# Hybrid decoder layer: another order of the mixer's projections, and the second half of the out-projection on VectorE

## The chip, the core and the metric

One Trainium2 chip, one core. The metric is the device time of one execution in microseconds; the median of three runs is given. The engines are TensorE (PE; PEld is its weight load), VectorE (DVE), ScalarE (ACT), GpSimd (POOL) and SyncE (SP), which issues the DMAs.

## The reference

All is float32; 512 tokens, width 1024. The layer is a SwiGLU FFN (half step), a mixer, and a second SwiGLU FFN:

```python
x = x + 0.5 * swiglu(rms_norm(x))                       # width 2816
proj = rms_norm(x) @ w_in                               # 1024 x 2560
xr, gate, q, k, v = split(proj, 512 columns each)
y_rnn = rg_lru(xr) * gelu(gate)                         # conv of 4, two block-diagonal gates, scan over time
q, k = rms_norm per head (8 heads of 64)
z = q @ k.T;  w = exp(log_sigmoid(z) + sum of log_sigmoid(-z) over later keys), causal
y_att = w @ v
y = concat(rms_norm(y_rnn), rms_norm(y_att))
x = x + y @ w_out
x = x + 0.5 * swiglu(rms_norm(x))
```

The recurrent half makes, for each channel, h[t] = a[t] h[t-1] + b[t] with a and b from two sigmoid gates of the convolved xr.

## The kernel before

Tokens lie along the free axis (512), channels on the 128 partitions, so x is eight tiles of 128x512. Each float32 matmul is three (`mm3`, lines 136 to 139): both operands are split into a rounded high part (ScalarE) and the rest (VectorE), and high x high, high x low and low x high are summed in a PSUM bank. `weights` loads a weight tile with one DMA from SP, then splits it; there are 3 buffers for the raw tile and 4 for each part. `Normed.add` splits x times a gain into `xh` and `xl`; the norm's factor is applied later, when the product is read. `Normed.square` has ScalarE square x and GpSimd add up the squares; four matmuls with a column of ones sum these over the partitions (`rsqrt`), and four transposes spread the result over a tile `rb` (`spread`).

The order in which each engine issues is made at build time by a planner: it goes through the program with a model of the engines, and of the instructions that the model has ready it takes the earliest in program order; `weights_early` moves an instruction 200 places forward. A tile with a tag takes one of that tag's buffers when its first instruction is placed, and one whose buffers are all held waits until one is released, while later instructions may pass it. `tc.issue_after(ins)` holds back, behind `ins`, the instructions of the block that are on the engine of `ins`, and no others.

In the mixer the eight PSUM banks are six with the tag "b" and two with the tag "y". `project(j)` makes block j of xr and gate (two banks "b", 48 matmuls); `convolve(j)` reads them, makes the convolution `xc`, its two parts `xch` and `xcl`, and the gelu `gel`; `gate(j)` makes the two gate products (6 matmuls, two banks) and the sigmoids from them. `recur` needs all four gates: exponentials, a square root, VectorE's scans, and a product on GpSimd into `gel`. `rnn_out` splits `gel` into `yrh` and `yrl`. `project_qkv` makes q, k or v for four groups of 128 tokens in four banks, 32 groups of three matmuls; after a given number of groups it calls what `between` says. For k the first two of the four banks have the tag "y". `norm_heads` norms the heads of q or k (square, sum, a power on GpSimd, a product into `nat`, which releases the bank), `turn` transposes `nat` on TensorE and splits it. The order before is: block 0, block 1, block 2, gate 0, block 3, gate 1, q with gates 2 and 3 inside, k with the recurrence and q's transposes inside, v with `rnn_out` and k's transposes inside.

In the attention, `weigh` makes scores and weights for a pair of heads, `turn_weights` transposes them, `attend` multiplies by v. The out-projection is made in two halves: `project_out(k, 0, ...)` for the recurrent half, put in between steps of the attention, and `project_out(k, 1, ...)` for the attention's half, for k = 0 to 7 at the end. Each is 12 matmuls, a product with `rb` on VectorE (`yo`, two buffers) and an addition into x[k] on GpSimd. After each of the second half, `done(k)` splits the new x[k] into `xh_b` and `xl_b` for the second FFN, whose banks take over those of the attention; last come the eight squares.

Of the kernel before, what the change touches and what calls it, by code (L numbers as in the profile page):

```python
# [8 lines left out]
F32 = mybir.dt.float32  # L9
F32R = mybir.dt.float32r  # L10
BF16 = mybir.dt.bfloat16
AF = mybir.ActivationFunctionType
# [3 lines left out]
P = 128  # L16
T = 512
D = 1024
KD = D // P
DFF = 2816  # L20
NF = DFF // P
DR = 512
# [27 lines left out]
def hybrid_layer_kernel(  # L50
# [17 lines left out]
    nc = tc.nc  # L68
# [21 lines left out]
    def bank(name, tag="b"):  # L90
        return banks["pool"].tile([P, T], F32, tag=tag, name=name, bufs=banks["tags"][tag])
# [25 lines left out]
    x = [xpool.tile([P, T], F32, tag=f"x{k}", name=f"x{k}") for k in range(KD)]  # L117


    def weights(src, name, n=KD * P):  # L120
        raw = wpool.tile([P, n], F32, tag="wr", name=f"r_{name}")
        nc.sync.dma_start(raw, src)
        return parts(raw, name, n)

    def parts(raw, name, n):
# [6 lines left out]
    def weights_early(*args):  # L132
        with tc.high_priority(offset=200):
            return weights(*args)
# [7 lines left out]
    class Normed:  # L142
# [5 lines left out]
        def add(self, xk, gain, j):  # L148
            n = self.name
            h = xpool.tile([P, T], F32R, tag="xh", name=f"xh_{n}{j}", bufs=8)  # L150
            nc.scalar.activation(h, xk, AF.Copy, scale=gain)
            l = xpool.tile([P, T], F32R, tag="xl", name=f"xl_{n}{j}", bufs=8)
            low = nc.vector.scalar_tensor_tensor(
                l, xk, gain, f32(h), op0=ALU.mult, op1=ALU.subtract
            )
            self.h[j], self.l[j] = h, l
            return low

        def square(self, xk, j):
            n = self.name  # L160
# [337 lines left out]
    rp = rnn.enter_context(tc.tile_pool(name="rnn", bufs=1, reuse_waits="tile"))  # L498
# [4 lines left out]
    def project(j, between=None):  # L503

        ws = [weights_early(w_rg[c], f"{n}{j}") for c, n in ((j, "xr"), (NJ + j, "ga"))]
        pts = [bank(f"p{n}{j}") for n in ("xr", "ga")]
        order = [(i, k) for i in range(2) for k in range(KD)]
        if j == 0:
            order = [(i, k) for k in ORDER for i in range(2)]
        for i, k in order:  # L510
            s = slice(k * P, (k + 1) * P)
            (wh, wl), ks = ws[i], [kk for ii, kk in order if ii == i]
            mm3(pts[i], wh[:, s], wl[:, s], nm.h[k], nm.l[k], k == ks[0], k == ks[-1])
            if between and (i, k) == order[KD - 1]:
                between()
        return pts

    def convolve(j, pr, pg):
        xr = rp.tile([P, T + 3], F32, tag="xr", name=f"xr{j}")
        nc.vector.memset(xr[:, 0:3], 0.0)  # L520
        nc.vector.tensor_mul(xr[:, 3:], pr, nm.rb)
        g = rp.tile([P, T], F32, tag=f"gel{j}", name=f"gel{j}")
        nc.vector.tensor_mul(g, pg, nm.rb)
        xc = rp.tile([P, T], F32, tag="xc", name=f"xc{j}", bufs=2)
        nc.gpsimd.tensor_scalar(
            xc, xr[:, 3:], v1(C_CW + 3 * NJ + j), v1(C_CB + j), op0=ALU.mult, op1=ALU.add
        )
        for w in range(3):
            nc.vector.scalar_tensor_tensor(
                xc, xr[:, w : w + T], v1(C_CW + w * NJ + j), xc, op0=ALU.mult, op1=ALU.add  # L530
            )
        xch = rp.tile([P, T], F32R, tag="xch", name=f"xch{j}", bufs=2)
        nc.scalar.copy(xch, xc)
        xcl = rp.tile([P, T], F32R, tag="xcl", name=f"xcl{j}", bufs=2)
        nc.vector.tensor_sub(xcl, xc, f32(xch))
        conv.append((xc, xch, xcl))

        g2 = rp.tile([P, T], F32, tag="g2", name=f"g2{j}")
        nc.scalar.activation(g2, g, AF.Square)
        k0 = 2.0 * (2.0 / 3.141592653589793) ** 0.5  # L540
        nc.gpsimd.tensor_scalar(g2, g2, k0 * 0.044715, k0, op0=ALU.mult, op1=ALU.add)
        nc.gpsimd.tensor_mul(g2, g2, g)
        nc.scalar.activation(g2, g2, AF.Sigmoid)
        nc.gpsimd.tensor_mul(g, g, g2)
        gel.append(g)

    def gate(j):
        xc, xch, xcl = conv[j]
        s = slice(j * P, (j + 1) * P)
        pa = bank(f"pa{j}")  # L550
        mm3(pa, bah[:, s], bal[:, s], xch, xcl, True, True)
        px = bank(f"px{j}")
        mm3(px, bxh[:, s], bxl[:, s], xch, xcl, True, True)

        nc.scalar.activation(dec[:, j, :], pa, AF.Sigmoid, bias=v1(C_BA + j))
        nc.scalar.activation(tau[:, j, :], dec[:, j, :], AF.Tanh, scale=half_c[:, j : j + 1])
        i = rp.tile([P, T], F32, tag=f"ix{j}", name=f"ix{j}")
        box["gate"] = nc.scalar.activation(i, px, AF.Sigmoid, bias=v1(C_BX + j))
        nc.gpsimd.tensor_mul(i, i, xc)
        ix.append(i)  # L560

    yrh, yrl = [], []
    box = {}

    yn = Normed("r")
# [36 lines left out]
    v = []  # L602
# [22 lines left out]
    def norm_heads(n, pts):  # L625
        nats = []
        for b in range(NB):
            rb = nm.r[:, b : b + 1]
            sq = rp.tile([P, DR], F32, tag="nsq", name=f"nsq{n}{b}", bufs=1)
            nc.scalar.activation(sq, pts[b], AF.Square, scale=rb)  # L630
            m = stat.tile([P, NH], F32, tag="m8", name=f"m8{n}{b}")
            nc.vector.tensor_reduce(m, heads(sq), axis=mybir.AxisListType.X, op=ALU.add)
            nc.vector.tensor_scalar(m, m, 1.0 / HD, EPS, op0=ALU.mult, op1=ALU.add)
            r = stat.tile([P, NH], F32, tag="r8", name=f"r8{n}{b}")
            nc.gpsimd.tensor_tensor(r, m, mhalf, op=ALU.pow)
            nat = rp.tile([P, DR], F32, tag=("xch", "xcl")[b % 2], name=f"nat{n}{b}", bufs=2)
            nc.vector.scalar_tensor_tensor(
                heads(nat),
                heads(pts[b]),
                rb,  # L640
                r.unsqueeze(2).to_broadcast([P, NH, HD]),
                op0=ALU.mult,
                op1=ALU.mult,
            )
            nats.append(nat)
        return nats
# [16 lines left out]
    pj = [project(0)]  # L663
# [2 lines left out]
    bah, bal = blockdiag(bd_a, "a")  # L666
    bxh, bxl = blockdiag(bd_x, "x")
    convolve(0, *pj[0])
    pj.append(project(2))
    convolve(1, *pj[1])  # L670
    gate(0)
    pj.append(project(3))
    convolve(2, *pj[2])
    gate(1)
    convolve(3, *pj[3])
    pq = project_qkv(0, "q", {8: lambda: gate(2), 16: lambda: gate(3)})
    nq = norm_heads("q", pq)
    pk = project_qkv(1, "k", {8: recur, 24: lambda: turn("q", nq)})
    nk = norm_heads("k", pk)
    pv = project_qkv(2, "v", {8: rnn_out, 27: lambda: turn("k", nk)})  # L680
    for b in range(NB):
        rb = nm.r[:, b : b + 1]
        v.append(mp.tile([P, DR], F32, tag=f"v{b}", name=f"v{b}", bufs=1))
# [3 lines left out]
    psum("att", z=4, w=3, y=1)  # L687


    def project_out(k, c, yh, yl, norm, tag, after=None):  # L690
        wh, wl = weights_early(w_out[k, :, c * DR : (c + 1) * DR], f"o{c}_{k}", DR)
        pt = bank(f"po{c}_{k}", tag)
        with tc.issue_after(after.ins) if after else nullcontext():
            for j in range(NJ):
                s = slice(j * P, (j + 1) * P)
                mm3(pt, wh[:, s], wl[:, s], yh[j], yl[j], j == 0, j == NJ - 1)
        tmp = ap.tile([P, T], F32, tag="yo", name=f"yo{c}_{k}", bufs=2)
        nc.vector.tensor_mul(tmp, pt, norm.rb)  # L698
        nc.gpsimd.tensor_add(x[k], x[k], tmp)

# [2 lines left out]
    with tc.tile_pool(name="att", bufs=2, reuse_waits="tile") as ap:  # L705
        beta = {}
        yah, yal = [], []
# [99 lines left out]

        yn.rsqrt(DR)
        yn.spread()
        project_out(0, 0, yrh, yrl, yn, "w")  # L810
        todo = 1
        ahead()
        ahead()
        for j, pair in enumerate(pairs):
            ws = []
            for h in pair:
                ws.append(ap.tile([P, 4 * W + P], F32, tag="wt", name=f"wt{h}", bufs=4))
            for qbs in ((3,), (2,), (1, 0)):
                for h, w in zip(pair, ws):
                    turn_weights(qbs, h, w)  # L820
                    if steps in WEIGH:
                        ahead()
                    if steps in FILL:
                        project_out(todo, 0, yrh, yrl, yn, "z")
                        todo += 1
                    steps += 1
            py = bank(f"py{j}", "y")
            attend(pair, py, ws)
            take(j, py)
        na.rsqrt(DR)  # L830
        na.spread()
        for k, step in zip(range(todo, KD), REST):
            project_out(k, 0, yrh, yrl, yn, "z", turns[step])
        n2 = Normed("b")
        done = into(n2, C_G2, squares=False)
        for k in range(KD):

            after = None if k < 2 else na.summed if k == 2 else na.spreading
            project_out(k, 1, yah, yal, na, "zw"[k % 2], after)
            done(k)  # L840
        with tc.issue_after(done.last.ins):
            for k in range(KD):
# [99 lines left out]
```

## Time and profile before

| what | us |
|---|---|
| median of three runs | 949.89 (949.12 to 950.03) |
| the profiled execution | 950.52 |
| its span, first to last instruction | 948.7 |
| TensorE busy | 927.4 |
| VectorE busy | 676.1 |
| ScalarE busy | 374.7 |
| GpSimd busy | 125.2 |

The mean granted clock of TensorE is 0.992 of its full rate. Busy time of TensorE counts overlapping matmuls once; a matmul of 512 columns is shown as 0.39 us but the next goes off earlier. The mixer lies between about 364 and 581 us: projections to 489, attention to 558, then the second half of the out-projection.

### The profile page before, as it was taken

How to read it: one execution, taken by the hardware profiler on the slowest of the kernel's cores; microseconds unless marked ns; L12 is line 12 of the kernel's file. 1: busy time of each engine (PE TensorE's matmuls, PEld its weight loads, DVE VectorE, ACT ScalarE, POOL GpSimd, SP SyncE). 2: the span in 40 equal slices, each digit the busy share in tenths (PEclk: the TensorE clock that was granted, in tenths of full speed). 3: DMA queues.
4: the chain of work that ended last, by engine and by line, in shares of the span. 5: the costliest groups of instructions: out<-in, count | busy, mean ns of one | idle time of the engine just before them, and what ended most of it. 6: DMA issues, size and time to landing. Idle time of an engine off the chain costs nothing.

```text
span 948.7 us, 12527 instructions
## 1 busy us (share of the span) xinstructions
PE 927.4 (98%) x4906; PEld 786.1 (83%) x4906; DVE 676.1 (71%) x997; ACT 374.7 (39%) x532; POOL 125.2 (13%) x87
## 2 busy tenths in 40 slices
PE   8999999999999999999899997999999999999998
PEld 6888988898889888888776575888988899889987
DVE  7687867686768559766859849287776777677753
ACT  7233333333333335446457546143333324233430
POOL 4000000000000005633802139100000000000000
PEclk9999999999999999999999998999999999999999
DMA  7430443035201513321110013421153125212312
GB/s 245 178 111 1 142 148 109 3 123 166 89 23 67 156 67 111 128 74 66 56 56 23 23 67 121 168 89 45 67 179 107 49 68 178 89 67 67 111 45 89
DMA packets 27131, 89.45 MB, mean 94 GB/s; under 512 B 3136, under 2 KB 5440, under 8 KB 27072
## 3 DMA queue, kind: packets, MB, share of 16 engines
q1 hardware_dynamic: 27072, 88.65, 27.2%
q8 instruction: 39, 0.64, 0.3%
q14 instruction: 20, 0.16, 0.1%
HBM read 86.54 MB, written 2.10 MB: 93 GB/s over the span
## 4 chain that ended last, share of the span: by engine, by line
PE 84%; DVE 7%; DMA 4%; issue 2%; POOL 1%; ACT 1%; SPq 0%; DVEq 0%; POOLq 0%; ACTq 0%
PE pdb L343 8%; PE pda L343 8%; PE pga L137 5%; PE pga L139 5%; PE pga L138 5%; PE pub L137 4%; PE pub L139 4%; PE pub L138 4%; PE pgb L137 4%; PE pgb L139 4%; PE pgb L138 4%; PE pua L137 4%; PE pua L138 4%; PE pua L139 4%; DVE rest L743 1%
## 5 line engine op out<-in xcount | busy, mean ns | idle before, releaser
L137 PE MATMUL pub<-xh_b,h_ub 128*128 128x512 f32 x176 | 69.2, 393 | 6.2 <-DVE yo L698 6.2
L343 PE MATMUL pda<-bha,l_da 128*128 128x256 f32 x252 | 70.5, 284 | 1.0 <-DVE l_da L129 1.0
L343 PE MATMUL pdb<-bhb,l_db 128*128 128x256 f32 x252 | 70.5, 284 | 0.9 <-DVE l_db L129 0.8
L343 PE MATMUL pdb<-bhb,h_db 128*128 128x256 f32 x252 | 71.3, 284 | 0.0
L343 PE MATMUL pda<-bha,h_da 128*128 128x256 f32 x252 | 71.2, 284 | 0.0
L343 PE MATMUL pda<-bla,h_da 128*128 128x256 f32 x252 | 71.0, 283 | 0.0
L343 PE MATMUL pdb<-blb,h_db 128*128 128x256 f32 x252 | 71.0, 283 | 0.0
L139 PE MATMUL pub<-xh_b,l_ub 128*128 128x512 f32 x176 | 69.0, 392 | 0.0
L138 PE MATMUL pub<-xl_b,h_ub 128*128 128x512 f32 x176 | 69.0, 392 | 0.0
L137 PE MATMUL pgb<-xh_b,h_gb 128*128 128x512 f32 x176 | 68.9, 392 | 0.0
L139 PE MATMUL pgb<-xh_b,l_gb 128*128 128x512 f32 x176 | 68.8, 391 | 0.0
L138 PE MATMUL pgb<-xl_b,h_gb 128*128 128x512 f32 x176 | 68.7, 391 | 0.0
L137 PE MATMUL pga<-xh_a,h_ga 128*128 128x512 f32 x160 | 62.4, 390 | 0.0
L137 PE MATMUL pua<-xh_a,h_ua 128*128 128x512 f32 x160 | 62.3, 390 | 0.0
L139 PE MATMUL pga<-xh_a,l_ga 128*128 128x512 f32 x160 | 62.3, 389 | 0.0
L138 PE MATMUL pga<-xl_a,h_ga 128*128 128x512 f32 x160 | 62.3, 389 | 0.0
L139 PE MATMUL pua<-xh_a,l_ua 128*128 128x512 f32 x160 | 62.3, 389 | 0.0
L138 PE MATMUL pua<-xl_a,h_ua 128*128 128x512 f32 x160 | 62.2, 389 | 0.0
L167 POOL TENSOR_TENSOR sqa_m<-sqa_m,sq_m 128x512 f32<-128x512 f32 x7 | 11.8, 1682 | 326.8 <-issue 322.9
L343 PEld LDWEIGHTS pda<-bha,l_da 128*128 128x128 f32 x252 | 47.9, 192 | 1.4 <-DVE l_da L129 1.4
L246 DVE TENSOR_TENSOR uub<-pub,rb_b 128x512 f32<-128x512 f32 x22 | 15.2, 690 | 47.3 <-PE pub L139 47.3
L343 PEld LDWEIGHTS pdb<-bhb,l_db 128*128 128x128 f32 x252 | 47.8, 192 | 1.3 <-DVE l_db L129 1.3
(316 smaller groups left out, 2474.3 us busy)
## 6 DMA issues: line engine op xcount, KB each, us to landing
r_gb<-in_wg SPq DMA_DIRECT2D x22, 512.0 KB, 3.2
r_ub<-in_wu SPq DMA_DIRECT2D x22, 512.0 KB, 3.3
r_ga<-in_wg SPq DMA_DIRECT2D x20, 512.0 KB, 3.2
r_ua<-in_wu SPq DMA_DIRECT2D x20, 512.0 KB, 3.6
rda<-in_wd SPq DMA_DIRECT2D x12, 768.0 KB, 5.1
rdb<-in_wd SPq DMA_DIRECT2D x12, 768.0 KB, 4.8
r_o<-in_w_out SPq DMA_DIRECT2D x16, 256.0 KB, 2.7
x<-in_xT SPq DMA_DIRECT2D x8, 256.0 KB, 4.5
```

Source lines behind the costliest of these rows:

```text
L137: nc.tensor.matmul(out_, wh, ah, start=start, stop=False)
L138: nc.tensor.matmul(out_, wh, al, start=False, stop=False)
L139: nc.tensor.matmul(out_, wl, ah, start=False, stop=stop)
L167: nc.gpsimd.tensor_add(self.acc, self.acc, sq)
L246: nc.vector.tensor_mul(u, pu, rb)
L343: nc.tensor.matmul(pt, p[:, s], a, start=start and i == 0 and q == 0, stop=i == m - 1 and q == 2, skip_group_check=True,)
L743: nc.vector.tensor_tensor_scan(rest[:, c : c + n - 1][:, ::-1], s[:, c + 1 : c + n][:, ::-1], zero.to_broadcast([P, n - 1]), 1.0, op0=ALU. ...
```

## The change

The projections run in the order block 0, block 1, q (with gates 0 and 1 inside), block 2, the transposes of q, block 3 (with gate 2 inside), k (with gate 3 and the recurrence inside, after eight groups), v (with `rnn_out` after twelve groups instead of eight, and k's transposes). The gates' banks have the tag "y" in place of "b". `nat` has a tag of its own with three buffers, in place of two each of `xch` and `xcl`. In the second half of the out-projection VectorE, not GpSimd, adds into x[k], and the weights of two k come with one DMA and are split in one go. `Normed.add` returns its ScalarE instruction, so that the last `issue_after` holds the eight squares behind the last `xh_b`.

```diff
-    def weights(src, name, n=KD * P):
+    def weights(src, name, n=KD * P, rows=1):
         raw = wpool.tile([P, n], F32, tag="wr", name=f"r_{name}")
-        nc.sync.dma_start(raw, src)
+        nc.sync.dma_start(raw if rows == 1 else raw.rearrange("p (k m) -> p k m", k=rows), src)
...
-            nc.scalar.activation(h, xk, AF.Copy, scale=gain)
+            high = nc.scalar.activation(h, xk, AF.Copy, scale=gain)
...
-            low = nc.vector.scalar_tensor_tensor(
+            nc.vector.scalar_tensor_tensor(
...
-            return low
+            return high
...
-        pa = bank(f"pa{j}")
+        pa = bank(f"pa{j}", "y")
...
-        px = bank(f"px{j}")
+        px = bank(f"px{j}", "y")
...
-            nat = rp.tile([P, DR], F32, tag=("xch", "xcl")[b % 2], name=f"nat{n}{b}", bufs=2)
+            nat = rp.tile([P, DR], F32, tag="nat", name=f"nat{n}{b}", bufs=3)
...
     convolve(0, *pj[0])
+    convolve(1, *pj[1])
+    pq = project_qkv(0, "q", {16: lambda: gate(0), 28: lambda: gate(1)})
+    nq = norm_heads("q", pq)
     pj.append(project(2))
-    convolve(1, *pj[1])
-    gate(0)
-    pj.append(project(3))
     convolve(2, *pj[2])
-    gate(1)
+    turn("q", nq)
+    pj.append(project(3, lambda: gate(2)))
     convolve(3, *pj[3])
-    pq = project_qkv(0, "q", {8: lambda: gate(2), 16: lambda: gate(3)})
-    nq = norm_heads("q", pq)
-    pk = project_qkv(1, "k", {8: recur, 24: lambda: turn("q", nq)})
+
+    def gate_and_recur():
+        gate(3)
+        recur()
+
+    pk = project_qkv(1, "k", {8: gate_and_recur})
     nk = norm_heads("k", pk)
-    pv = project_qkv(2, "v", {8: rnn_out, 27: lambda: turn("k", nk)})
+    pv = project_qkv(2, "v", {12: rnn_out, 27: lambda: turn("k", nk)})
...
-        nc.gpsimd.tensor_add(x[k], x[k], tmp)
+        (nc.vector if c else nc.gpsimd).tensor_add(x[k], x[k], tmp)
+
+    def weights_out(k, c, n):
+
+        src = w_out[k : k + n, :, c * DR : (c + 1) * DR].rearrange("k p m -> p k m")
+        wh, wl = weights_early(src, f"o{c}_{k}", n * DR, n)
+        return [[p[:, i * DR : (i + 1) * DR] for p in (wh, wl)] for i in range(n)]
...
-            project_out(k, 1, yah, yal, na, "zw"[k % 2], after)
+            if k % 2 == 0:
+                two = weights_out(k, 1, 2)
+            project_out(k, 1, yah, yal, na, "zw"[k % 2], two[k % 2], after)
```

## Rows read from the trace of the kernel before

**Rows 1.** The page, part 1: busy time, share of the span, instructions.

```profile
PE 927.4 (98%) x4906; PEld 786.1 (83%) x4906; DVE 676.1 (71%) x997; ACT 374.7 (39%) x532; POOL 125.2 (13%) x87
```

**Rows 2.** TensorE's waits: line waited for, total us, times, longest.

```profile
PE pub L137 <- DVE yo L698: 6.2, 1, 6.2
...
PE ptq L653 <- DVE natq L637: 2.8, 1, 2.8
```

**Rows 3.** Timeline of the projections: start us, us, engine, line, operation.

```profile
387.35 0.39 PE L137 MATMUL pxr<-xh_m,h_xr 128*128 128x512 f32 x1
...
398.23 0.40 PE L137 MATMUL pa<-xch,bdha 128*128 128x512 f32 x1
...
452.92 0.60 PE L653 MATMUL ptq<-ident,natq 128*128 128x128 f32 x4
...
488.70 1.02 PE L174 MATMUL pst_r<-ones,sqa_r 128*128 128x1 f32 x8
```

**Rows 4.** Timeline of TensorE between the mixer and the second FFN.

```profile
581.58 0.39 PE L139 MATMUL pgb<-xh_b,l_gb 128*128 128x512 f32 x1
...
588.16 0.77 PE L137 MATMUL pub<-xh_b,h_ub 128*128 128x512 f32 x1 [6.19 <-DVE yo L698]
...
592.14 0.45 PE L137 MATMUL pgb<-xh_b,h_gb 128*128 128x512 f32 x1
```

**Rows 5.** Busy us by stretch: length, PE, PEld, DVE, ACT, POOL, clock, DMA.

```profile
464.90:488.70 23.80, 23.80 (x115) 19.68 (x113) 14.12 (x23) 11.15 (x18) 6.49 (x4) 1.00 0.13 44
557.70:568.30 10.60, 10.60 (x54) 8.89 (x53) 3.88 (x7) 3.58 (x7) 3.93 (x3) 1.00 0.27 97
581.80:588.20 6.40, 0.21 (x2) 0.07 (x1) 6.40 (x7) 3.27 (x5) 6.40 (x4) 0.78 0.45 160
588.20:592.10 3.90, 3.90 (x9) 3.11 (x10) 3.90 (x3) 1.35 (x2) 3.90 (x3) 0.50 0.03 11
```

**Rows 6.** Timeline of the other engines in the out-projection's second half.

```profile
567.70 0.59 ACT L198 COPY rb_t<-psr_t 128x512 f32<-128x512 f32 x1
...
572.51 0.61 ACT L166 ACTIVATE sq_b<-x 128x512 f32<-128x512 f32 x1
...
584.63 2.24 POOL L699 TENSOR_TENSOR x<-x,yo 128x512 f32<-128x512 f32 x1
...
587.34 0.68 DVE L698 TENSOR_TENSOR yo<-po,rb_t 128x512 f32<-128x512 f32 x1
```

**Rows 7.** Groups by line, 566 to 592 us: busy us, mean ns.

```profile
L699 POOL TENSOR_TENSOR x<-x,yo 128x512 f32<-128x512 f32 x8 | 14.4, 1822 | 3.1 <-DVE yo L698 3.1
L153 DVE SCALAR_TENSOR_TENSOR xl_b<-x,vec,xh_b 128x512 fp32r<-128x512 f32 x7 | 11.2, 1593 | 0.0
L167 POOL TENSOR_TENSOR sqa_b<-sqa_b,sq_b 128x512 f32<-128x512 f32 x5 | 9.2, 1834 | 0.0
```

**Rows 8.** One tile, the weights' low part: ns least/median/most.

```profile
L129 DVE TENSOR_TENSOR l_o<-r_o,h_o x16: 680/686/1158, 475.9 to 571.1; 128x512 fp32r<-128x512 f32 x16
```

**Rows 9.** Timeline of the recurrence: last gate, last gel, first use.

```profile
426.80 0.39 PE L139 MATMUL px<-xch,bdlx 128*128 128x512 f32 x1
...
451.74 2.54 POOL L583 TENSOR_TENSOR gel<-gel,tau 128x512 f32<-128x512 f32 x2
...
489.58 0.48 PE L137 MATMUL po<-yrh,h_o 128*128 128x512 f32 x1
```

**Rows 10.** Single tiles: ns least/median/most, first and last start.

```profile
L637 DVE SCALAR_TENSOR_TENSOR natk<-pk,r_m,r8k x4: 744/750/752, 466.9 to 473.5; 128x512 f32<-128x512 f32 x4
...
L635 POOL TENSOR_TENSOR r8k<-m8k,mhalf x4: 1634/1638/1647, 464.9 to 471.8; 128x8 f32<-128x8 f32 x4
...
L583 POOL TENSOR_TENSOR gel<-gel,tau x4: 1287/1786/3187, 443.8 to 453.0; 128x512 f32<-128x512 f32 x4
...
L590 DVE SCALAR_TENSOR_TENSOR yrl<-gel,vec,yrh x4: 746/749/752, 474.6 to 477.2; 128x512 fp32r<-128x512 f32 x4
...
L733 PE MATMUL pz<-fut_b,ident_b x8: 219/224/230, 493.4 to 497.2; 128*128 128x128 bf16 x8
```

More of the change, by code (lines that the diff above doesn't have):

```diff
@@ L687, in hybrid_layer_kernel, with project_out @@
     psum("att", z=4, w=3, y=1)
-    def project_out(k, c, yh, yl, norm, tag, after=None):
-        wh, wl = weights_early(w_out[k, :, c * DR : (c + 1) * DR], f"o{c}_{k}", DR)
+    def project_out(k, c, yh, yl, norm, tag, ws, after=None):
+        wh, wl = ws
         pt = bank(f"po{c}_{k}", tag)
@@ L809, in hybrid_layer_kernel @@
         yn.spread()
-        project_out(0, 0, yrh, yrl, yn, "w")
+        project_out(0, 0, yrh, yrl, yn, "w", *weights_out(0, 0, 1))
         todo = 1
@@ L823, in hybrid_layer_kernel @@
                     if steps in FILL:
-                        project_out(todo, 0, yrh, yrl, yn, "z")
+                        project_out(todo, 0, yrh, yrl, yn, "z", *weights_out(todo, 0, 1))
                         todo += 1
@@ L832, in hybrid_layer_kernel @@
         for k, step in zip(range(todo, KD), REST):
-            project_out(k, 0, yrh, yrl, yn, "z", turns[step])
+            project_out(k, 0, yrh, yrl, yn, "z", *weights_out(k, 0, 1), turns[step])
         n2 = Normed("b")
```

## The prediction

> **What bounds the kernel now.** I read the page's busy shares first, then TensorE's waits, then the timeline around each wait, and last what the other engines did there. TensorE is busy 98% of the span, so only its gaps, and matmuls at the lower clock, can give time back [rows 1]. Two of its waits lie where the edits are: 6.2 us at the first up-projection of the second FFN, 2.8 us at the transposes of q [rows 2].
>
> Both cost more than the wait, because the granted clock falls behind them. A matmul of 512 columns normally goes off every 0.227 us: 48 of one block from 387.35 to 398.23 [rows 3]. From 387.35 to 488.70 TensorE issues 408 of them (two blocks 96, four gates 24, q, k and v 288) and 32 transposes: 408 x 0.227 = 92.5, plus eight groups of four transposes at 0.60 = 4.8, together 97.3. The stretch takes 101.35 [rows 3], so **4.0 us are lost in the projections**: the wait of 2.8, the rest slow matmuls. At the second wait the last matmuls of the out-projection and the first three of the FFN go off until 581.58; the next could follow at 581.81 and follows at 588.16. Nine more steps go by until 592.14, at a granted clock of 0.50 (1.2 GHz) [rows 4, 5]. Idle 6.35, slow part 3.98 - 9 x 0.227 = 1.94: **8.3 us are lost between the mixer and the second FFN**.
>
> What ends last there is GpSimd. VectorE is full in 581.8 to 588.2 (6.40 of 6.40), but GpSimd is too [rows 5], and it sets the beat: one addition into x (2.24 us) and one sum of squares (1.8 us) per block make about 4 us, against 12 x 0.227 = 2.7 of TensorE; with two `yo` buffers the yo of block 7 waits for the addition of block 5, and TensorE starts when that yo (587.34) is over [rows 6, 7]. VectorE's busy time is swollen: xl_b means 1593 ns here, an operation of its kind and size 750 ns elsewhere [rows 7, 10].
>
> **The second half of the out-projection.** Eight additions leave GpSimd (8 x 1.82 = 14.6 us) and come to VectorE. The trace has no such addition on VectorE; the nearest two-input instruction of 128x512 takes 0.68 us without GpSimd beside it and 1.16 at most [rows 8]. I take 0.69, since GpSimd will be empty. The squares now queue behind the last xh_b on ScalarE; the old edge named a VectorE instruction and held none of them back, as the square at 572.51 shows [rows 6]. So GpSimd has nothing to sum until the last x is split. Its seven sums (1.8 each, 13 us) and ScalarE's squares (0.61 each, 5 us) then lie beside the products of two blocks, 96 x 0.227 = 21.8 us of TensorE, ahead of the reduction that needs them: no cost while they end by then; if they did not, other products can go first.
>
> VectorE then needs, for each of eight blocks, yo 0.68 + addition 0.69 + xl_b 0.75 = 2.12 us. It can't begin before rb_t is there, at 567.70 + 0.59 = 568.29 [rows 6], when three blocks are already waiting. Block 7's yo comes at 568.3 + 7 x 2.12 = 583.1 and ends at 583.8, with nothing else in between. Pairing turns eight weight loads, copies and subtractions into four of twice the size, all beside matmuls: I count nothing for it. But four weight buffers now hold all eight blocks, so they can be split before 568.3, where VectorE is busy 3.88 of 10.6 [rows 5]. If one pair and the first gate and up weights fall behind 568.3 all the same, that is three subtractions at not more than twice 0.68, 4.1 us, and the last yo ends at 587.9.
>
> The bank of the up product is the one that waited for the last yo. If that stays, TensorE waits until 583.8 to 587.9 and the slow clock stays: a gain of 0.3 to 4.4. But the planner orders the queue by its own model, and with the additions on VectorE that model has the backlog in it; it then has eight groups of gate products (3 x 0.227 = 0.68 each, 5.4 us) to put in front. So the other end is the full 8.3. xl_b allows it: block 7's is done at 586 to 590, and TensorE, which starts at 581.1 and spends 1.36 on each, reaches it at 590.6. I take **-6.3**, nearer the upper end.
>
> The Trainium skill speaks against this move ("Perfetto Trace Analysis", Optimizing Scalar/DVE Operations): where VectorE is saturated, moving work off it to ScalarE or even GpSimd may help, so loading a full VectorE should not. By that rule the last yo comes at its late end and the gain is nearer 0.3. The same section adds that both engines share an SBUF read port, so that moving work between them might not help; xl_b at twice its length fits the sharing, and by it VectorE's full stretch is partly waiting.
>
> **The order of the projections.** It becomes two blocks, q, two blocks, k, v. q's norm chain then has a whole block (10.9 us) to run in and the transposes find it done: the 4.0 us go. q's four banks are the two that no block has used and the two of block 0, which block 3 took over before, only later; I count no wait. The three `nat` buffers make the fourth part of q (and of k) wait until the first is transposed; other matmuls cover the 2 us.
>
> The price is the recurrence. Its last gate is written behind the first eight groups of k, and its two banks now have the tag "y", of which there are two; k's first two parts hold both until they are normed. So gate 3 can't run where it stands. Counting on from 387.35: q with two gates, 108 matmuls, to 411.8; block 2 to 422.7; transposes 425.1; block 3 with gate 2 to 437.4; k's first part is complete after 26 of its 32 groups, at 455.1. Its norm is a square, a sum and a scaling (no row of mine: twice 0.75 and 0.2), the power on GpSimd 1.64 and the product 0.75 [rows 10]: 4.1, with four hand-overs some 4.6. The second part follows 1.7 later, since there is one buffer for the square. Gate 3 ends at about 462, against 426.80 + 0.39 = 427.2: 35 us later [rows 9]. Before, the last gel came 27.1 us after it (451.74 + 2.54 = 454.28), yrh and yrl take 1.5, and the first to use them was a matmul at 489.58 [rows 9, 10]. Now yrl comes at 462 + 27.1 + 1.5 = 490.7, while v ends at 459.1 + 1.4 + 21.8 + 2.4 = 484.7. What had over 30 us of slack is **6.0 us late**.
>
> TensorE has the first attention scores for that time, whose masks lay from 493.4 to 497.2 [rows 10], some 4 us, if k's transposes are split soon enough. VectorE is busy 14.12 of 23.8 us in the stretch of v [rows 5] and gets some 10 of recurrence: full at its end, and the attention starts behind that. Bounds: -4.0 (all covered) to +5 (the 6.0 waited, the clock down behind it for 1.9 as in [rows 5], 1 for a further stall in the attention, less 4.0). I take **-2.0**.
>
> Sum: 950.5 (the profiled execution; the median shown is 0.6 less) - 6.3 - 2.0 = 942.2, so **941.6** for the median.
>
> **Rivals.**
> - *Both losses go whole*: the scores cover the late recurrence, and TensorE never waits for the last yo. -4.0 - 8.3: 937.6. For it: TensorE has work of other stages in reach at both places. Against: VectorE's count above. 0.20.
> - *VectorE takes GpSimd's place*: the up product still waits for the last yo, which ends at 586; gain 2, mixer -2: 945.9. For it: the same bank, and the backlog from 568.3. Against: gate products can be put in between. 0.20.
> - *The late recurrence sets the end* (slower): the change does not put it where the code says, and the planner has the first out-projection ahead of the scores, so that TensorE stands at it. The lateness is 6.0 with gel as long as before; with each gel at its longest, 3.19 against 1.29 at its shortest [rows 10], four times, it is 13.6. At 11, with 1.9 of slow clock, less 4.0, that is +8.9; less 6.3, +2.6: 952.5. It decides from 6.3 + 4.0 - 1.9 = 8.4 us of lateness on. Against: the planner's model knows of the bank. 0.12.
> - *Nothing to see*: mixer +4, second part -4: 949.9. 0.06.
>
> **How the numbers follow.** The forecast has 0.42, with its own range 938.5 to 945. The whole range reaches from the best case, less 1 for what else may shorten, to just under no change: 936.5 to 949. A change under 0.2% can't be told from none here. Faster by more: 0.42 + 0.20 + 0.20 = 0.82; same 0.06; slower 0.12.
>
> **What would show it.** TensorE waits no more for natq; the last gate's matmuls come behind most of k (if they stand within its first third, my reading of the banks is wrong and the mixer can gain the whole 4.0); yrl ends behind v. In the out-projection GpSimd is empty until the last xh_b, xl_b is near 0.75, the additions near 0.69, and TensorE's gap ahead of the second FFN is under 3 us, with gate products in front. The forecast falls if that gap stays above 5 us, or if a new gap above 6 us stands at the first out-projection.

## The result: slower by 0.5%, by the wait that the forecast thought covered

| what | before | after |
|---|---|---|
| median of five runs, us | 949.12 (948.47 to 950.03) | 953.68 (952.60 to 955.15) |
| ratio to before, 95% interval | | 1.0047 (1.0033 to 1.0062) |
| profiled execution, us | 950.52 | 952.85 |

The forecast was 941.6, within 936.5 to 949.0, and the time is above both. At 950 us the ratio is +4.5 us; the two profiled executions, from which the rows below come, are 2.3 us apart. The page's busy shares after the change (as in [rows 1]) show nothing of it: TensorE has 98% again, only GpSimd is busy 14 us less, eight additions.

```profile
PE 928.4 (98%) x4906; PEld 787.1 (83%) x4906; DVE 675.0 (71%) x1001; ACT 375.2 (39%) x529; POOL 111.1 (12%) x79
```

TensorE's waits after (line waited for, total us, times, longest) correspond to [rows 2]. Both waits of before are gone or nearly so (0.5 of 6.2 is left, none of 2.8), and one of 10.3 us stands at the transposes of k, with another of 1.1 at the sum of the attention's squares.

```profile
PE ptk L653 <- DVE kTl L659: 10.3, 1, 10.3
...
PE pst_t L174 <- POOL sqa_t L167: 1.1, 1, 1.1
...
PE pub L137 <- DVE yo L702: 0.5, 1, 0.5
```

Where the time went by stage is read from the four column sums of the norms (line 174), since each of them ends a stage: `pst_m` opens the mixer, `pst_r` ends the projections, `pst_t` the attention with the first half of the out-projection, `pst_b` the second half and the second FFN's first products. The last column of a row gives its first and last start. First before, then after:

```profile
L174 PE MATMUL pst_m<-ones,sqa_m x8: 164/250/250, 375.1 to 375.8; 128*128 128x1 f32 x8
L174 PE MATMUL pst_r<-ones,sqa_r x8: 242/250/250, 488.7 to 489.5; 128*128 128x1 f32 x8
L174 PE MATMUL pst_t<-ones,sqa_t x8: 164/250/250, 563.4 to 564.1; 128*128 128x1 f32 x8
L174 PE MATMUL pst_b<-ones,sqa_b x8: 164/250/250, 611.3 to 611.9; 128*128 128x1 f32 x8
```

```profile
L174 PE MATMUL pst_m<-ones,sqa_m x8: 164/250/250, 374.2 to 374.9; 128*128 128x1 f32 x8
L174 PE MATMUL pst_r<-ones,sqa_r x8: 213/352/352, 494.1 to 495.5; 128*128 128x1 f32 x8
L174 PE MATMUL pst_t<-ones,sqa_t x8: 250/250/271, 574.0 to 574.8; 128*128 128x1 f32 x8
L174 PE MATMUL pst_b<-ones,sqa_b x8: 164/250/250, 614.4 to 615.1; 128*128 128x1 f32 x8
```

The lengths of these stages (us), with those of the experiments below; "rest" is from `pst_b` to the end:

| kernel | projections | attention | second half | rest |
|---|---|---|---|---|
| before | 113.6 | 74.7 | 47.9 | 337.4 |
| after | 119.9 | 79.9 | 40.4 | 336.7 |
| e2, the order alone | 119.9 | 79.5 | 48.1 | 337.9 |
| e10, the order alone, gate 3 on "b" | 109.0 | 74.6 | 48.0 | 336.6 |
| e1, the second half alone | 113.6 | 77.2 | 42.0 | 336.5 |
| e11, the second half alone, single weights | 113.6 | 75.0 | 41.5 | 337.4 |
| e3, after with gate 3 on "b" | 109.0 | 75.5 | 42.0 | 336.6 |
| e12, after with yrl behind k's split | 116.2 | 78.0 | 42.0 | 336.6 |

So the second half gave back 7.5 us in its own stage (5.9 to 6.4 where it stands alone), and the projections lost 6.3, the attention 5.2.

**The projections.** TensorE's timeline corresponds to [rows 3, 9]. Gate 3's two products go off at 462.83 and 465.60 and end at 466.47, where the forecast had 462. The last product of v goes off at 481.74 (the forecast had its end at 484.7). Then TensorE stands until k's last eight transposes at 492.40; the first out-projection follows at 495.70, the first scores at 500.01.

```profile
462.83 0.40 PE L137 MATMUL pa<-xch,bdha 128*128 128x512 f32 x1
...
465.60 0.40 PE L137 MATMUL px<-xch,bdhx 128*128 128x512 f32 x1
...
481.74 0.39 PE L139 MATMUL pv<-h_v,xl_m 128*128 128x512 f32 x1
...
492.40 1.94 PE L653 MATMUL ptk<-ident,natk 128*128 128x128 f32 x8 [10.27 <-DVE kTl L659]
...
495.70 0.77 PE L137 MATMUL po<-yrh,h_o 128*128 128x512 f32 x1
...
498.76 0.40 PE L138 MATMUL po<-yrl,h_o 128*128 128x512 f32 x1
...
500.01 0.50 PE L734 MATMUL pz<-kTh,qTh 64*128 64x512 f32 x2
```

k's first two banks were free earlier than that: their norms end at 458.26 and 461.09, and gate 3's products follow 4.6 and 4.5 us later, put by the planner's order among products of v, with TensorE busy all the time.

```profile
457.51 0.75 DVE L637 SCALAR_TENSOR_TENSOR natk<-pk,r_m,r8k 128x512 f32<-128x512 f32 x1 [0.24 <-POOL r8k L635]
...
460.35 0.74 DVE L637 SCALAR_TENSOR_TENSOR natk<-pk,r_m,r8k 128x512 f32<-128x512 f32 x1
```

What the transposes wait for is in VectorE's timeline. In the order that the planner wrote, `kTl`, the low part of k's first two transposes, stands behind all four `yrl`. These need `gel` from GpSimd; VectorE does not stand idle for it here but is full without a break, and beside GpSimd one `yrl` takes 1.75 us instead of 0.75 [rows 10].

```profile
483.21 3.35 DVE L590 SCALAR_TENSOR_TENSOR yrl<-gel,vec,yrh 128x512 fp32r<-128x512 f32 x2
486.49 1.75 DVE L129 TENSOR_TENSOR l_o<-r_o,h_o 128x512 fp32r<-128x512 f32 x1
488.16 1.75 DVE L590 SCALAR_TENSOR_TENSOR yrl<-gel,vec,yrh 128x512 fp32r<-128x512 f32 x1
489.84 0.74 DVE L637 SCALAR_TENSOR_TENSOR natk<-pk,r_m,r8k 128x512 f32<-128x512 f32 x1
490.50 1.09 DVE L590 SCALAR_TENSOR_TENSOR yrl<-gel,vec,yrh 128x512 fp32r<-128x512 f32 x1
491.51 1.40 DVE L659 SCALAR_TENSOR_TENSOR kTl<-ptk,vec,kTh 128x512 fp32r<-128x512 f32 x2
```

GpSimd's timeline has the last two products into `gel`, then the sums of their squares, without a pause until 491.04:

```profile
482.25 3.76 POOL L583 TENSOR_TENSOR gel<-gel,tau 128x512 f32<-128x512 f32 x2 [1.76 <-DVE tau L580]
485.99 5.05 POOL L167 TENSOR_TENSOR sqa_r<-sqa_r,sq_r 128x512 f32<-128x512 f32 x3
```

The stretches (length; PE, PEld, DVE, ACT, POOL busy; clock; DMA share, GB/s) say the same: VectorE and ScalarE full, TensorE empty, and its granted clock about half in the next ten microseconds too, which is its lower level of 1.2 GHz for part of them.

```profile
484.70:490.00 5.30, 0.00 (x0) 0.00 (x0) 5.30 (x5) 5.30 (x10) 5.14 (x4) 0.53 0.12 35
490.00:500.00 10.00, 7.60 (x28) 6.53 (x28) 5.17 (x8) 2.21 (x5) 2.06 (x2) 0.57 0.11 36
```

**The second half** gained what was forecast. The groups of the stretch 574 to 596 us (busy us, mean ns) correspond to [rows 7]: the additions, never seen on VectorE before, take 680 ns (forecast 690), xl_b 740 instead of 1593. GpSimd has no work from 580 to 590. Three gate products stand in front of the up product, as many as before [rows 4]; TensorE waits 0.54 for the last `yo`, and the nine steps behind that wait take 2.17 us instead of 3.98.

```profile
L703 DVE TENSOR_TENSOR x<-x,yo 128x512 f32<-128x512 f32 x8 | 5.4, 680 | 0.0
...
L153 DVE SCALAR_TENSOR_TENSOR xl_b<-x,vec,xh_b 128x512 fp32r<-128x512 f32 x6 | 4.4, 740 | 0.0
```

```profile
591.84 0.39 PE L137 MATMUL pgb<-xh_b,h_gb 128*128 128x512 f32 x1
...
593.22 0.50 PE L137 MATMUL pub<-xh_b,h_ub 128*128 128x512 f32 x1 [0.54 <-DVE yo L702]
...
595.39 0.39 PE L137 MATMUL pgb<-xh_b,h_gb 128*128 128x512 f32 x1
```

### The profile page after: what moved, and what is told of

Read it like the earlier page. It is cut to its first block, busy times and chain, and to the rows that moved or that the text cites. A ratio compares the mean times of both kernels' runs of the same rounds, so it can differ in the third digit from the quotient of the medians.

```text
span 951.1 us, 12503 instructions
## 1 busy us (share of the span) xinstructions
PE 928.4 (98%) x4906; PEld 787.1 (83%) x4906; DVE 675.0 (71%) x1001; ACT 375.2 (39%) x529; POOL 111.1 (12%) x79
## 4 chain that ended last, share of the span: by engine, by line
PE 87%; DVE 6%; DMA 3%; issue 1%; ACT 1%; SPq 1%; POOL 0%; DVEq 0%; ACTq 0%
PE pda L343 9%; PE pdb L343 8%; PE pga L137 5%; PE pga L139 5%; PE pga L138 5%; PE pub L137 4%; PE pub L139 4%; PE pgb L137 4%; PE pub L138 4%; PE pgb L139 4%; PE pgb L138 4%; PE pua L137 4%; PE pua L139 4%; PE pua L138 4%; PE po L137 1%
## 5 line engine op out<-in xcount | busy, mean ns | idle before, releaser
L343 PEld LDWEIGHTS pda<-bha,h_da 128*128 128x128 f32 x252 | 48.3, 192 | 0.5
```

The lines of the kernel that those rows point to most:

```text
L343: nc.tensor.matmul(pt, p[:, s], a, start=start and i == 0 and q == 0, stop=i == m - 1 and q == 2, skip_group_check=True,)
```

## The experiments

Each time stands beside runs of the kernel before on the same chip (medians 949.71 to 950.45 in the three batches); the ratios have 95% intervals. "us by the ratio" is at 950.

| kernel | median us | ratio | us by the ratio |
|---|---|---|---|
| e1 | 945.52 | 0.9961 (0.9946 to 0.9976) | -3.7 |
| e2 | 960.04 | 1.0105 (1.0087 to 1.0123) | +10.0 |
| e3 | 939.10 | 0.9886 (0.9869 to 0.9903) | -10.8 |
| e4 | 953.62 | 1.0043 (1.0028 to 1.0058) | +4.1 |
| e5 | 954.52 | 1.0038 (1.0021 to 1.0056) | +3.6 |
| e6 | 950.48 | 1.0003 (0.9990 to 1.0016) | +0.3 |
| e7 | 948.91 | 0.9983 (0.9973 to 0.9993) | -1.6 |
| e8 | 937.93 | 0.9869 (0.9854 to 0.9885) | -12.4 |
| e10 | 943.48 | 0.9939 (0.9922 to 0.9956) | -5.8 |
| e11 | 942.29 | 0.9924 (0.9911 to 0.9938) | -7.2 |
| e12 | 946.76 | 0.9971 (0.9960 to 0.9983) | -2.8 |
| e13 | 936.81 | 0.9860 (0.9843 to 0.9877) | -13.3 |

### Each half of the change alone: e1 and e2

e1 has the new second half with the old order, gate banks and `nat`; e2 the reverse.

```diff
e1, against after:
-    pk = project_qkv(1, "k", {8: gate_and_recur})
+    pk = project_qkv(1, "k", {8: recur, 24: lambda: turn("q", nq)})
... (and the rest of the old order, banks and nat)
e2, against after:
-        (nc.vector if c else nc.gpsimd).tensor_add(x[k], x[k], tmp)
+        nc.gpsimd.tensor_add(x[k], x[k], tmp)
... (and single weights, the squares' old edge)
```

> The kernel before with only the second half of the out-projection changed (VectorE adds, paired weights, squares behind the last xh_b); the projections and banks stay as before. Theory A (the two parts of the change act apart; the projections alone cost): the stretch from the sum over the attention's squares to the one over x's squares takes 40.6 us as in the changed kernel, 7.4 less than before, and the time is 949.1 - 7.4 = 941.7. Rival B (the second half only looked short because the attention before it ended late and let VectorE catch up): under 3 us gained, 946 or more.

> The kernel before with only the order of the projections changed (with the gates' banks, the nat buffers and rnn_out as in the changed kernel). Theory A: the wait of some 10 us at k's transposes and the slow clock behind it are there as in the changed kernel; 949.1 + 10.6 = 959.7, or a little less. Rival B (the loss needs both parts): between 949 and 953.

The order alone costs 10.0 us, the second half alone gives 3.7. That makes +6.3 against +4.5 of both, within what the intervals leave. In e2 TensorE's waits are the 10.3 of the changed kernel and the 6.2 of the one before, so each wait belongs to one half of the change:

```profile
PE ptk L653 <- DVE kTl L659: 10.3, 1, 10.3
PE pub L137 <- DVE yo L702: 6.2, 1, 6.2
```

e1 gives only 3.7 of the 6.3 that the second half was to give, though its wait at the up product is 0.5, and its 945.5 lies between its two expectations: its second half is 5.9 shorter than before (7.4 were expected), and its attention 2.5 longer. That was open, and e6 to e8 and e11 go into it.

### The place of gate 3: e3 and e10

```diff
-        pa = bank(f"pa{j}", "y")
+        pa = bank(f"pa{j}", "b" if j == 3 else "y")
-        px = bank(f"px{j}", "y")
+        px = bank(f"px{j}", "b" if j == 3 else "y")
```

e3 makes this edit in the changed kernel, e10 in e2, whose second half is that of before.

> The changed kernel with the last gate's two banks from the six with the tag b. Theory A (the bank that the last gate lacks makes the recurrence late, and its VectorE work then stands in front of k's transposes): the last gate runs about 443, 20 us earlier, TensorE waits for k's transposes under 2 us, and the time is 953.7 - 12 = 938 to 942. Rival C (VectorE has too much in the stretches of k and v in this order, wherever the gate stands, or the fourth nat buffer is missing): a wait of over 5 us stays, 947 or more.

> The kernel before with the new order of the projections alone, and gate 3's two products on banks of the tag b instead of y; the second half of the out-projection as before. Theory A (the late last gate alone makes the loss in the projections, and the two edits add up): the order alone cost 10.4 with gate 3 on y (960.0 against 949.6), and putting it on b took 14.6 off the changed kernel (953.7 to 939.1), so here 945.5, between 944 and 947: the 4.0 us that were lost in the projections are gained whole. TensorE has no wait at the transposes of q or k, and still 6 us at the first up product. Rival J (the order gains only together with the second half): 948.5 to 950.5.

One gate on other banks takes 15.3 us off the changed kernel, by the two ratios (1.0047 and 0.9886). Gate 3 then stands where the code puts it, 25 us earlier:

```profile
440.56 0.40 PE L137 MATMUL px<-xch,bdhx 128*128 128x512 f32 x1
```

TensorE waits neither at k's nor at q's transposes, in e10 as in e3; the projections take 109.0 us in both, 4.6 less than before, where the forecast had 4.0 to gain. The order by itself was worth its gain; the two banks turned it into a loss. e10 is below its expected 944 to 947 by half a microsecond, which its interval covers.

### What TensorE waits for behind the late gate: e4, e5 and e12

e4 gives `nat` a fourth buffer (one of `xch`), against the reading that k's fourth part, at 489.84, is what is late. e5 and e12 move `rnn_out` in program order behind k's transposes; e12 also holds `yrl` on VectorE behind the last `kTl`.

```diff
e4:
-            nat = rp.tile([P, DR], F32, tag="nat", name=f"nat{n}{b}", bufs=3)
+            nat = rp.tile([P, DR], F32, tag="nat" if b < 3 else "xch", name=f"nat{n}{b}", bufs=3 if b < 3 else 2)
e5:
-    pv = project_qkv(2, "v", {12: rnn_out, 27: lambda: turn("k", nk)})
+    pv = project_qkv(2, "v", {27: lambda: turn("k", nk), 28: rnn_out})
e12, with the order of e5 (turned[0] is the last kTl):
-            nc.vector.scalar_tensor_tensor(
-                l, gel[j], v1(C_RN + j), f32(h), op0=ALU.mult, op1=ALU.subtract
-            )
+            with tc.issue_after(turned[0].ins):
+                nc.vector.scalar_tensor_tensor(
+                    l, gel[j], v1(C_RN + j), f32(h), op0=ALU.mult, op1=ALU.subtract
+                )
```

> The changed kernel with a fourth buffer for nat (the fourth one takes a buffer of xch). Theory A (the wait at k's transposes is that for the split of the first two, which stands behind the recurrence in VectorE's queue): the fourth natk comes early, but the wait stays above 6 us; 951 to 954. Rival D (k's fourth norm, waiting for the first transpose, is what VectorE's queue is late with): the wait falls below 3 us and the time to 946 or less.

> The changed kernel with rnn_out written behind k's transposes, so that the split of k comes before the split of the recurrence in the program; the last gate is as late as in the changed kernel. Theory A (VectorE's queue holds the splits of the late recurrence, and l_o, in front of kTl): the wait at k's transposes falls from 10.3 to 3 to 6 us, but TensorE then finds the first out-projection late, so that only part comes back; 947 to 951. Rival E (the order within that queue does not matter, since the recurrence itself is what TensorE waits for): 952 to 955.

> The changed kernel with the low parts of the recurrence's output held on VectorE behind the last low part of k. Theory A (TensorE stands at k's last transposes because VectorE, an engine that takes its instructions in order, has the late recurrence ahead of k's split): the wait there falls from 10.3 us to 3 or 4 (k's high part on ScalarE still stands behind the last yrh), the first scores go off at about 492 instead of 500, and the time is 945.5 to 949. Rival L (it is GpSimd and VectorE themselves that are late, so the wait only moves to the sum of the recurrence's squares and the first out-projection): 951 to 955, and TensorE's waits at these two make up for what goes.

With four buffers k's last part is normed at 464.2, 26 us earlier, and TensorE still waits 10.2 us: `nat` is not it.

```profile
L637 DVE SCALAR_TENSOR_TENSOR natk<-pk,r_m,r8k x4: 742/751/751, 457.8 to 464.2; 128x512 f32<-128x512 f32 x4
```

e5 missed: its wait is 10.3 as ever, since its VectorE queue has `yrl` ahead of `kTl` all the same (by the planner's rule its model had `yrl` ready first; the place in the program did not overrule that). Its time lies in the rival's range, 952 to 955, but it tested nothing of the queue; e12 does. There `kTl` goes off at 487.44 instead of 491.51, k's last transposes at 488.34 instead of 492.40, the first scores at 492.98 instead of 500.01. The wait falls to 6.2 (3 or 4 were expected), and the time by 7.3 us by the two ratios, inside what was expected of the queue's order and below the rival's 951. The profiled execution of e12, 948.86, is the slowest of its eleven.

```profile
487.44 1.41 DVE L660 SCALAR_TENSOR_TENSOR kTl<-ptk,vec,kTh 128x512 fp32r<-128x512 f32 x2 [1.86 <-ACT kTh L659]
```

What is left of the wait looks like the same fault on ScalarE: k's high part stands directly behind the last `yrh`, which needs GpSimd's last `gel`, over at 486.05, though k's first transposes go off from 477.7 on. Moving that one too was not tried, so this is read from the rows and not shown.

```profile
486.12 0.71 ACT L588 ACTIVATE yrh<-gel,vec 128x512 fp32r<-128x512 f32 x1
486.74 1.25 ACT L659 ACTIVATE kTh<-ptk,vec 128x512 fp32r<-128x512 f32 x2
```

### The second half, edit by edit: e6, e7, e8, e11, e13

e6 and e7 make one edit each in the kernel before: VectorE adds, or the squares stand behind the last `xh_b`. e8 is e3 and e11 is e1 with the weights of the second half one k at a time. e13 is e8 with VectorE adding the last three blocks of the first half as well.

```diff
e6: -        nc.gpsimd.tensor_add(x[k], x[k], tmp)
    +        (nc.vector if c else nc.gpsimd).tensor_add(x[k], x[k], tmp)
e7: -            return low
    +            return high
e8, e11:
-            if k % 2 == 0:
-                two = weights_out(k, 1, 2)
-            project_out(k, 1, yah, yal, na, "zw"[k % 2], two[k % 2], after)
+            project_out(k, 1, yah, yal, na, "zw"[k % 2], *weights_out(k, 1, 1), after)
e13, from e8:
-        (nc.vector if c else nc.gpsimd).tensor_add(x[k], x[k], tmp)
+        (nc.vector if c or k >= 5 else nc.gpsimd).tensor_add(x[k], x[k], tmp)
```

> The kernel before with nothing changed but the engine of the second half's eight additions into x (VectorE). Theory F (GpSimd's beat of addition and sum of squares is what TensorE waits for, and moving the additions breaks it alone): the gap ahead of the second FFN falls from 6.2 to under 2 us, 943 to 946. Rival G (the sums of squares, still among the blocks, slow VectorE as before and it now has more to do): the gap stays above 4 us, 948 to 951.

> The kernel before with nothing changed but the place of the eight squares (behind the last xh_b on ScalarE); the additions stay on GpSimd. Theory F (GpSimd's beat): with one addition of 1.7 to 2.2 us per block GpSimd keeps up with TensorE's 2.7, the gap falls under 2 us, 943 to 946. Rival G (the additions themselves are the late ones, with their collisions with VectorE): the gap stays above 4 us, 948 to 951.

> The changed kernel with the last gate's banks from the tag b (which gave 939.1) and the second half's weights loaded and split one by one. Theory H (pairing cost something: the split of two blocks' weights, 1.22 us on VectorE, lies beside GpSimd's last addition of the first half, which takes 2.2 in place of 1.66, and TensorE waits 1.1 us for the sum behind it and then runs at the lower clock): that wait goes, 936 to 938. Rival I (pairing is free or saves): 939 to 941.

> The kernel before with the second half of the out-projection changed alone, but its weights one k at a time: VectorE adds, and the squares stand behind the last high part. Theory H (pairing makes the new wait of 1.1 us ahead of the second half and brings nothing): 943.5 to 945.2 (945.5 with pairs, less 1.2 as between the two kernels with gate 3 on b), TensorE has no wait at the sum over the attention's squares. Rival K (pairing is what gets the weights split in time, so the additions need it): 946.5 or more, the wait at the first up product back above 3 us.

> The fastest kernel so far (gate 3 on b, single weights, 937.9) with VectorE also adding the last three blocks of the first half into x, so that GpSimd has fewer additions ahead of the sum of the attention's squares. Theory M (that sum's wait is gone there already, nothing else hangs on those additions): 937.3 to 938.6. Rival N (GpSimd's additions still delay the chain to the attention's norm): 936 to 937.2. Rival G (VectorE, full there, is slowed by them): 939 or more.

Neither edit is enough alone, and both times lie in the range of the rival (948 to 951): e6 gives nothing, e7 1.6 us. With the additions on VectorE but GpSimd still summing squares beside them (e6), the additions take 816 ns on the mean and xl_b 1105, and the wait is 6.9; with the squares away but the additions on GpSimd (e7), xl_b takes 1254 and the wait is 4.9. With both, in e11, GpSimd has nothing to do beside VectorE, and all three of its instructions per block have the length that the forecast gave them. The groups of e6, e7 and e11, in this order:

```profile
L153 DVE SCALAR_TENSOR_TENSOR xl_b<-x,vec,xh_b 128x512 fp32r<-128x512 f32 x8 | 8.8, 1105 | 0.6 <-ACT xh_b L151 0.6
L699 DVE TENSOR_TENSOR x<-x,yo 128x512 f32<-128x512 f32 x8 | 6.4, 816 | 0.0
```

```profile
L153 DVE SCALAR_TENSOR_TENSOR xl_b<-x,vec,xh_b 128x512 fp32r<-128x512 f32 x8 | 9.9, 1254 | 0.2 <-ACT xh_b L151 0.2
```

```profile
L153 DVE SCALAR_TENSOR_TENSOR xl_b<-x,vec,xh_b 128x512 fp32r<-128x512 f32 x8 | 5.8, 744 | 0.2 <-ACT xh_b L151 0.2
L698 DVE TENSOR_TENSOR yo<-po,rb_t 128x512 f32<-128x512 f32 x8 | 5.3, 682 | 0.0
L699 DVE TENSOR_TENSOR x<-x,yo 128x512 f32<-128x512 f32 x8 | 5.2, 681 | 0.0
```

On pairing, e11 is 3.5 us below e1 by the ratios, with intervals that don't meet; e8 is 1.6 below e3, but there they overlap, so on that side no difference is shown. The forecast had counted nothing. Pairs shorten the last wait (0.5 at the up product against 1.7 in e11 and e8), and pay at the sum of the attention's squares, `pst_t`: GpSimd's last addition of the first half starts when its `yo` is over, VectorE's next instruction is a weight split, and the two lie beside each other. In e1 that is a pair of 1.22 us, the addition takes 2.20, the sum behind it ends at 564.42, and TensorE waits 1.1 for it, with six slow steps (0.43) from 566.94 on; in e11 the split is 0.68, the addition 1.66, and TensorE does not wait. That wait is half of the 2.2 us by which the attention of e1 is longer than e11's; what the other half is stays open. In e3, which has the wait, and e8, which has not, the attention takes 75.5 us both, but in the profiled execution of e8 twelve steps of it, from 496.70 on, are slow ones, which is 2.5 us that e3 does not have. GpSimd's and VectorE's rows, e1 first:

```profile
560.83 1.22 DVE L129 TENSOR_TENSOR l_o<-r_o,h_o 128x1024 fp32r<-128x1024 f32 x1
...
560.99 2.20 POOL L699 TENSOR_TENSOR x<-x,yo 128x512 f32<-128x512 f32 x1 [5.38 <-DVE yo L698]
563.15 1.27 POOL L167 TENSOR_TENSOR sqa_t<-sqa_t,sq_t 128x512 f32<-128x512 f32 x1
```

```profile
558.51 0.68 DVE L129 TENSOR_TENSOR l_o<-r_o,h_o 128x512 fp32r<-128x512 f32 x1
...
558.67 1.66 POOL L699 TENSOR_TENSOR x<-x,yo 128x512 f32<-128x512 f32 x1 [3.78 <-DVE yo L698]
```

e11 is 1.2 below the least that its expectation gave. e13 has the lowest median of all, and its 936.81 lies in the range of rival N, but its interval and e8's overlap. Of their stages only the attention differs by more than 0.6 us (74.3 in e13 against 75.5), and e8's twelve slow steps there, against three in e13, are more than that, so those three additions are not shown to matter. e8 and e13 beat both kernels: 12 to 13 us faster than before.

## Why the prediction was wrong

**The loss that it started from, and the order's gain: right.** 4.0 us in the projections were to go with q's wait; 4.6 go in e3 and e10.

**The lateness: right in mechanism, small in size.** The banks with the tag "y" hold gate 3 back, as forecast (e3). The last `yrl` ends at 491.59 against 490.7, v ends at 482.1 against 484.7: late by 9.5 instead of 6.0. That 490.7 came out so near is luck, since two errors nearly cancel. k's two banks came free when counted (458.26 and 461.09, where 455.1 + 4.6 and 1.7 more give 459.7 and 461.4), but gate 3 stands further back in TensorE's order and ends 4.5 us late; from its end to the last `yrl` it takes 25.1 us, where 27.1 + 1.5 were counted.

**The step that failed** is the term of -2.0 for the order of the projections, and in it the sentence that TensorE has the first scores for that time, "if k's transposes are split soon enough". They were not. The forecast counted VectorE's work in the stretch of v as a sum (14.12 of 23.8 us, and some 10 of recurrence) and asked whether it fits; it did not ask what stands ahead of k's split in the queues of VectorE and ScalarE. There the late recurrence lies, so that lateness isn't covered by the scores but held in front of them: 10.3 us at the transposes. All of it goes when gate 3 is early (e3, e10), and e12 shows that 4.1 of it are VectorE's order alone; the rest was not taken apart by a run. The measured term is +10.0 (e2) in place of -2.0, and the stated bounds (-4 to +5) did not hold it. 15.8 us lie between e2 and e10, which differ in gate 3's banks alone.

Of these, 10.9 lie in the projections (119.9 against 109.0) and 4.9 in the attention. For the changed kernel and e3 the attentions are 4.4 apart. Seven steps of the first out-projection take 3.06 instead of 1.59 (495.70 to 498.76 above), the slow clock behind the wait: 1.5. TensorE is idle 0.7 more (80.00 - 74.76 against 75.50 - 70.92, the length and TensorE's busy time of the two attentions, after and e3). Eight further slow steps, 1.6 us more than at the full clock, stand far behind, from 542.89 on, as steps of that kind do in the kernel before (535.32), in e10 (529.86), in e11 (534.44) and in e8 (496.70) but not in e3; that these come from the lateness is not shown. The rest, 0.6, is not assigned.

**The slower rival was the nearest**, at 952.5: the first out-projection does stand ahead of the scores, and the lateness of 9.5 is past its point of 8.4. It put the wait one step too late, at the out-projection rather than at k's transposes, and had 0.12. That its time is so near is in part luck: it had its lateness from long products into `gel`, up to 3.19 each, and they took 1.71 to 2.11.

**The second half: right in size, for the version without pairs, and partly by another way.** -6.3 was forecast, e11 gives -7.2, of which 6.4 in its own stage. The additions' length, the empty GpSimd and xl_b's return to 0.74 came. The further gate products in front, on which the upper end rested, did not: three stand there as before, in the changed kernel and in e11. TensorE still waits for the last `yo`, only short (0.54 and 1.71 us), and its granted clock behind that wait is 1.00 (nine steps in 2.17 us, above), where the lower end had counted the slow clock. That the number came so near is thus in part luck.

The reading that GpSimd sets the beat was wrong as well. In the kernel before, block 5's addition is over at 582.99, 4.35 us before block 7's `yo` starts (587.34). VectorE waits for GpSimd's additions only 0.81 us, and from 570.49 on it is full: what is late is VectorE's own work, stretched by GpSimd beside it. So e6, which takes the additions from GpSimd, leaves the wait at 6.9.

```profile
570.49 0.69 DVE L698 TENSOR_TENSOR yo<-po,rb_t 128x512 f32<-128x512 f32 x1 [0.81 <-POOL x L699]
...
580.75 2.24 POOL L699 TENSOR_TENSOR x<-x,yo 128x512 f32<-128x512 f32 x1
```

"I count nothing for it", for pairing, failed: beside GpSimd a split of twice the length delays an addition on the way to the attention's norm, and e1 and e11 are 3.5 us apart, of which the wait behind that addition is 1.1.

The rule that the forecast weighed, of the Trainium skill, "Perfetto Trace Analysis", Optimizing Scalar/DVE Operations, speaks of moving work off a saturated VectorE; read the other way round, as the forecast read it, the move onto a full one would bring next to nothing. e6 agrees with that (no change), e11 doesn't (-7.2): VectorE's full stretch was in part waiting (xl_b 1593 ns before, 744 in e11), and that goes only when GpSimd has nothing else to do there either.

## What to carry to other kernels

When a step is made late, don't ask only whether the engines have room for it: list, in the queue of each engine that its successors use, what stands behind them, because unrelated work there is late as well. A tag with few buffers moves an instruction further than its place in the program does, so look first at who holds the buffers. And where VectorE and GpSimd slow each other, judge edits together: two that gave nothing (e6) and 1.6 us (e7) alone gave 7.2 together (e11).

## What was not expected of the hardware

VectorE and GpSimd delay each other whichever came first, by nearly the length of the overlap. An addition on GpSimd took 1.28 us with VectorE idle or starting later, 1.66 beside a split of 0.68 us of which 0.52 were left (0.38 more), 2.20 beside one of 1.22 of which 1.06 were left (0.92 more); the split of 1.22 us took 2.35 when that addition had begun first (below), 1.13 more. The Trainium skill, "SBUF — State Buffer", Who interferes with whom, says that a VectorE instruction with two SBUF inputs contends with a GpSimd instruction that reads SBUF, and describes the shared ports as an exclusive lock; these rows agree. An instruction of VectorE that takes its large input from a PSUM bank was not stretched: `natk<-pk` takes 0.74 at 489.84 beside GpSimd's sums, as it does without them [rows 10].

The rows of that addition and of the split that took 2.35 us, GpSimd's and VectorE's in e1:

```profile
554.33 1.28 POOL L699 TENSOR_TENSOR x<-x,yo 128x512 f32<-128x512 f32 x1 [2.94 <-DVE yo L698]
```

```profile
554.35 2.35 DVE L129 TENSOR_TENSOR l_o<-r_o,h_o 128x1024 fp32r<-128x1024 f32 x1
```
